# A two-layer decoder trunk: second-layer scores and transposes moved from the whole TensorE array to its 64-row halves

## The chip, the cores and the metric

The kernel runs on one core of one Trainium2 chip. The metric is the device time of one execution in microseconds (us), less being better. Instructions run on five engines: TensorE (PE in the profile, its weight loads PEld), VectorE (DVE), ScalarE (ACT), GpSimd (POOL) and SyncE (SP), which here issues all DMAs.

## The reference

Two layers work on 2048 tokens of width 1024, with 16 learned meta tokens in front. The first is sliding-window attention with sinks beside a convolution branch. The second, which the change is about, is stick-breaking attention with 16 heads of size 64:

```python
def stick_breaking_attention(q, k, v):
    ...
    scale = d ** -0.5
    for i in range(nb):                       # blocks of 128 queries
        kend = (i + 1) * BLOCK
        z = jnp.einsum('bqhd,bkhd->bhqk', qp[:, i * BLOCK:kend], kp[:, :kend]) * scale
        valid = (kpos >= META_PAD) & (kpos < qpos)
        log_beta = jax.nn.log_sigmoid(z)
        log_1m = jnp.where(valid, jax.nn.log_sigmoid(-z), 0.0)
        after = lax.cumsum(log_1m, axis=3, reverse=True) - log_1m
        a = jnp.where(valid, jnp.exp(log_beta + after), 0.0)
        outs.append(jnp.einsum('bhqk,bkhd->bqhd', a, vp[:, :kend]))
...
def stick_breaking_mixer(h, w_in, w_out):
    q, k, v, g = _split(h @ w_in, SB_SPLITS)
    o = stick_breaking_attention(...)
    return (o * jax.nn.silu(g)) @ w_out
```

Each layer adds its normalised output to its input.

## The kernel before

**Precision.** Matmuls take fp32 data. A large product is made of rounded parts: an operand x is split into xh (rounded, "fp32r") and the rest xl. `mm3` (lines 137 to 139) makes one product from three matmuls, xh yh + xh yl + xl yh. Projections, in both layers, are 24 matmuls for each unit of up to 512 tokens, in one PSUM bank (`pj`).

**The second layer** takes pairs of heads p = 0..7, and halves of the sequence hf = 0, 1. `proj(p, hf)` makes q, k, v and the gate for a pair and writes them to device memory; `attn(p, hf)` reads them back. `interleave` weaves the steps of `attn` for one pair into those of `proj` for a later one. Within `attn`, `start` loads k and v (tiles `kst`, `vt1`), `group` opens an accumulator `av` for 512 queries, `qload(m)` loads the queries of a pair of tiles (256 queries, `qt`), `chunk` works on one stretch of up to four key blocks for these 256 queries and both heads, and `finish` adds the meta tokens' values and multiplies by the gate.

One `chunk`, for each head h and each query tile x of 128:
- scores: head size 64 fills only half of the array's 128 rows, so `kst` holds kh in rows 0 to 63 and kl in rows 64 to 127, and `qt` holds qh twice, or ql twice. Two matmuls over all 128 rows (L928) make (qh + ql)(kh + kl) in a bank `z`;
- ScalarE makes sigmoid(-z/8) (`om`, L935) and sigmoid(z/8) (`be`, L936); VectorE forms the running product from the right (L941) and multiplies it into `be` (L942); GpSimd sets edge columns and masks;
- transposes: each 128x128 block of `be` is transposed by TensorE (L960) into a bank `pt`, four blocks to a bank; ScalarE copies the bank to `aT` (L966);
- values: `aT` is multiplied by v (L974) into `av`, head 0 in the partitions 0 to 63, head 1 in 64 to 127. As fp32 matmuls they run as two instructions each.

**PSUM.** Eight banks: PB = (2, 3, 2) for `pj`, `pz` (scores, and transposes elsewhere) and `pt`, and one for `av`. In the first layer projections alternate between `pj` and `pz`; in the second they use `pj` alone.

**What sets the order.** The program is written engine by engine by a scheduler, which simulates the program as recorded and places each instruction when its operands are due; `high_priority` moves the value matmuls forward, `issue_after` (in `behind`) holds projections behind earlier value matmuls. The engines then run in that fixed order, each waiting on semaphores. Of instructions that are recorded side by side, the one whose bank or operand is free first can come first.

Of the kernel before, what the change touches and what calls it, by code (L numbers as in the profile page):

```python
# [18 lines left out]
P = 128  # L19
# [18 lines left out]
PB = (2, 3, 2)  # L38
# [42 lines left out]
class Trunk:  # L81
# [105 lines left out]
    def layer0(self, after=None):  # L187
# [319 lines left out]
        def cbranch(ut):  # L507
# [44 lines left out]
            def pw():  # L552
# [3 lines left out]
                for m in range(4):  # L556
                    if m % 2 == 0:
                        wh, wl = self.weights(pwset, a["w_pw2"][m // 2], lambda: w2.tile([P, KB, P], F32, tag="yl", name="raw", bufs=1), f"wp{m // 2}")
                    ps = self.bank("pj", "pw")
# [87 lines left out]
        def outp(t):  # L647
# [3 lines left out]
            def mm(nh):  # L651
# [9 lines left out]
                ps = self.bank("pj", "po")  # L661
# [92 lines left out]
    def after0(self, pool, tags):  # L754
        self.layer1_pools()
        self.evs = (pool, tags, D, 2)
        self.H, self.gates, self.tags = {}, [], cycle(("raw", "wh", "wl", "wh", "wl"))
# [9 lines left out]
        def proj(p, hf, parts=(0, 1)):  # L767
# [11 lines left out]
            def unit(m, part, c0, n, evac):  # L779
                def go():  # L780
# [4 lines left out]
                    ps = self.bank("pj", "pj1")  # L785
# [54 lines left out]
    def layer1(self):  # L840
# [12 lines left out]
        def attn(p, hf):  # L853
# [43 lines left out]
            def qload(m):  # L897
                q0 = NM + m * 2 * P
                S["q"] = qs = []
                for h in range(2):  # L900
                    for i in range(2):
                        qt = w2.tile([P, 256], F32R, tag=f"q{h}{i}", name="qt")
                        for j in range(2):
                            self.mv(qt[j * HD : j * HD + HD], qd[i][p, h * HD : h * HD + HD, q0 : q0 + 256])
                        qs.append(qt)

            def pair_steps(m):
# [5 lines left out]
                def chunk(ei):  # L913
# [7 lines left out]
                    for h in range(2):  # L921
                        for x in range(2):
                            n = nbs[x] * P + mo
                            if n == 0:
                                continue
                            z = self.bank("pz", "z")
                            for i in range(2):
                                nc.tensor.matmul(z[:, :n], S["q"][2 * h + i][:, x * P : x * P + P], S["k"][h][:, k0 : k0 + n], start=(i == 0), stop=(i == 1))  # L928
# [7 lines left out]
                            nc.scalar.activation(be[:, :n], z[:, :n], AF.Sigmoid, scale=0.125)  # L936
# [11 lines left out]
                    for c in range(0, b1 - b0, 2):  # L948
                        cw = min(2, b1 - b0 - c)
                        aTs = []  # L950
                        for h in range(2):
                            pt = self.bank("pt", "pt1")
                            lo, hi = None, 0
                            for b in range(c, c + cw):
                                for x in range(2):
                                    if b < nbs[x]:
                                        o = (b - c) * 256 + x * P
                                        lo = o if lo is None else lo
                                        hi = max(hi, o + P)
                                        nc.tensor.transpose(pt[:, o : o + P], bes[h, x][:, mo + b * P : mo + b * P + P], self.ident)  # L960
                            aT = w4.tile([P, 512], F32, tag="aT", name="aT")
                            if nbs[0] < c + cw and cw == 2:
                                nc.scalar.copy(aT[:, :256], pt[:, :256])
                                cps.append(nc.scalar.copy(aT[:, 384:512], pt[:, 384:512]))
                            else:
                                cps.append(nc.scalar.copy(aT[:, lo:hi], pt[:, lo:hi]))  # L966
                            aTs.append(aT)
# [182 lines left out]
```

## Time and profile before

| | us |
|---|---|
| median of 3 runs | 2894.17 (2893.23 to 2900.21) |
| the profiled execution | 2898.19 |
| its span, first to last instruction | 2896.5 |
| TensorE busy | 2740.0 (95%) |
| VectorE busy | 2171.0 (75%) |
| ScalarE busy | 1466.1 (51%) |
| GpSimd busy | 753.9 (26%) |
| mean granted TensorE clock | 0.981 |

How to read the lines of a profile below. The page gives, for each engine, busy time, share of the span and count of instructions. A group of instructions reads: line, engine, operation, output<-inputs, partitions x elements, xcount | busy us, mean ns of one | idle time of the engine before them and what ended it. Matmuls overlap in their pipeline, so a group's count times its mean is more than its busy time; where one follows the next, the pace is the distance between their starts or ends. In the timeline a row has its start and its duration in us, and neighbours of the same kind are merged with their count. "128*128" is the part of the array that a matmul uses: rows by columns. In a row by windows come the stretch, its length, and each engine's busy us with its instructions in brackets (PE, PEld, DVE, ACT, POOL), then TensorE's granted clock, the DMA engines' busy share, and GB/s. A row of waits says who waited for whom: us in total, times, the longest.

### The profile page before, as it was taken

To read this page: it belongs to the slowest core of one execution; us is meant where nothing else is said; L and a number is where in the kernel's file an instruction comes from. 1 tells how busy PE (TensorE), PEld (TensorE's weight loads), DVE (VectorE), ACT (ScalarE), POOL (GpSimd) and SP (SyncE) were. 2 spreads that over 40 slices of the span, in tenths; PEclk is the share of its full clock that TensorE was granted. 3 is DMA by queue.
4 is the path that set the end of the run, shared out by engine and by line. 5 is a ranking of instruction groups with operands and counts; after the bars stand their busy time and mean duration, and the time that the engine had idled before them with its cause. 6 is when DMAs were issued, how large, how long until landed. Compare 5 with 4: busy or idle time off the path is not lost.

```text
span 2896.5 us, 49247 instructions
## 1 busy us (share of the span) xinstructions
PE 2740.0 (95%) x16110; PEld 2199.4 (76%) x16110; DVE 2171.0 (75%) x3448; ACT 1466.1 (51%) x3568; POOL 753.9 (26%) x2663
## 2 busy tenths in 40 slices
PE   6999899998999999999999899999999999989997
PEld 6888677876777798888887677767777777766876
DVE  4899679886757743666668987888888887887864
ACT  4211344335646323545545666666666666665551
POOL 4222201010000212333335532323233222333210
PEclk9999999999989999999999999999999999999999
DMA  6665767668757664444446462323233342243332
GB/s 243 222 206 189 233 186 232 195 216 256 224 181 203 204 195 141 136 125 129 136 134 185 126 176 74 103 80 97 68 102 92 85 111 74 73 135 121 113 95 91
DMA packets 294191, 433.49 MB, mean 150 GB/s; under 512 B 45552, under 2 KB 199552, under 8 KB 290864
## 3 DMA queue, kind: packets, MB, share of 16 engines
q1 hardware_dynamic: 293936, 430.34, 49.4%
q8 instruction: 129, 2.11, 0.3%
q14 instruction: 126, 1.03, 0.1%
HBM read 282.80 MB, written 142.14 MB: 147 GB/s over the span
## 4 chain that ended last, share of the span: by engine, by line
PE 73%; DVE 8%; DMA 6%; ACT 4%; issue 4%; POOL 2%; SPq 1%; DVEq 0%; ACTq 0%; POOLq 0%
PE pj L137 12%; PE pj L138 11%; PE pj L139 11%; PE z L928 8%; PE av L974 7%; PE pt L960 7%; PE po L137 4%; PE po L138 4%; PE po L139 4%; DVE S L941 2%; DVE y L308 1%; DVE be L942 1%; DMA qs<-qr 1%; PE av L990 1%; ACT be L936 1%
## 5 line engine op out<-in xcount | busy, mean ns | idle before, releaser
L941 DVE TENSOR_TENSOR_SCAN S<-om,be 128x401 f32<-128x401 f32 (+3 forms) x512 | 536.8, 1070 | 72.7 <-ACT om L935 51.6
L935 ACT ACTIVATE om<-z 128x384 f32<-128x384 f32 (+5 forms) x768 | 379.1, 512 | 202.0 <-PE z L928 130.3
L942 DVE TENSOR_TENSOR be<-be,S 128x385 f32<-128x385 f32 (+5 forms) x768 | 415.3, 566 | 77.3 <-POOL be L933 22.1
L137 PE MATMUL pj<-th,wh 128*128 128x512 f32 (+2 forms) x1280 | 461.2, 360 | 6.7 <-DVE ev L826 4.0
L139 PE MATMUL pj<-th,wl 128*128 128x512 f32 (+2 forms) x1280 | 454.0, 355 | 0.0
L138 PE MATMUL pj<-tl,wh 128*128 128x512 f32 (+2 forms) x1280 | 451.7, 353 | 0.0
L966 ACT COPY aT<-pt 128x512 f32<-128x512 f32 (+2 forms) x672 | 334.7, 505 | 192.8 <-PE pt L960 153.2
L928 PE MATMUL z<-kst,qt 128*128 128x384 f32 (+6 forms) x1536 | 395.5, 358 | 31.4 <-ACT be L936 30.1
L936 ACT ACTIVATE be<-z 128x384 f32<-128x384 f32 (+5 forms) x768 | 376.8, 507 | 72.7 <-PE pt L960 72.1
L960 PE MATMUL pt<-ident,be 128*128 128x128 f32 x2176 | 363.1, 281 | 19.4 <-ACT ev L815 7.7
L308 DVE SCALAR_TENSOR_TENSOR y<-u,cw,y 128x1040 f32<-128x1040 f32 (+1 forms) x240 | 339.6, 1415 | 3.4
L960 PEld LDWEIGHTS pt<-ident,be 128*128 128x128 f32 x2176 | 252.9, 141 | 114.8 <-ACT aT L966 31.7
L137 PE MATMUL pj<-hTh,wh 128*128 128x512 f32 (+2 forms) x880 | 318.0, 362 | 14.4 <-DVE gt L387 5.5
L139 PE MATMUL pj<-hTh,wl 128*128 128x512 f32 (+2 forms) x880 | 315.1, 359 | 6.5 <-POOL wl L127 5.2
L138 PE MATMUL pj<-hTl,wh 128*128 128x512 f32 (+2 forms) x880 | 315.1, 358 | 2.3 <-DVE hTl L185 2.3
L928 PEld LDWEIGHTS z<-kst,qt 128*128 128x128 f32 x1536 | 248.4, 191 | 76.0 <-ACT be L936 55.5
L974 PE MATMUL av<-aT,vt 128*64 128x256 f32 (+1 forms) x2304 | 279.1, 377 | 4.3 <-DVE og L992 4.3
L932 POOL MEMSET om<- 128x1 f32 x768 | 74.0, 98 | 772.6 <-DVE S L941 757.6
L137 PEld LDWEIGHTS pj<-th,wh 128*128 128x128 f32 x1280 | 242.3, 189 | 33.7 <-DVE ev L826 4.9
L139 PEld LDWEIGHTS pj<-th,wl 128*128 128x128 f32 x1280 | 241.3, 189 | 30.2 <-DVE wl L112 0.3
L138 PEld LDWEIGHTS pj<-tl,wh 128*128 128x128 f32 x1280 | 241.9, 189 | 25.4 <-issue 0.4
L941 DVE TENSOR_TENSOR_SCAN S<-om 128x257 f32<-128x257 f32 (+4 forms) x256 | 204.8, 811 | 62.1 <-POOL om L939 49.3
(190 smaller groups left out, 4471.3 us busy)
## 6 DMA issues: line engine op xcount, KB each, us to landing
raw<-in_w_in SPq DMA_DIRECT2D x98, 512.0 KB, 4.1
wh<-wk SPq DMA_DIRECT2D x38, 512.0 KB, 4.7
wl<-wk SPq DMA_DIRECT2D x38, 512.0 KB, 5.9
qt<-qhd SPq DMA_DIRECT2D x256, 64.0 KB, 2.6
qt<-qld SPq DMA_DIRECT2D x256, 64.0 KB, 2.4
wk<-wh SPq DMA_DIRECT2D x22, 512.0 KB, 3.2
wk<-wl SPq DMA_DIRECT2D x22, 512.0 KB, 3.8
kst<-khd SPq DMA_DIRECT2D x16, 516.0 KB, 7.2
```

The costliest lines, as they stand in the source:

```text
L137: mm(out, sh, mh, start=first, stop=False)
L138: mm(out, sh, ml, start=False, stop=False)
L139: mm(out, sl, mh, start=False, stop=last)
L308: return lambda: nc.vector.scalar_tensor_tensor(y[:, :TW], u[:, w : w + TW], cw[:, j, w : w + 1], y[:, :TW], ALU.mult, ALU.add)
L928: nc.tensor.matmul(z[:, :n], S["q"][2 * h + i][:, x * P : x * P + P], S["k"][h][:, k0 : k0 + n], start=(i == 0), stop=(i == 1))
L935: nc.scalar.activation(om[:, :n], z[:, :n], AF.Sigmoid, scale=-0.125)
L936: nc.scalar.activation(be[:, :n], z[:, :n], AF.Sigmoid, scale=0.125)
L941: nc.vector.tensor_tensor_scan(P_[:, : n + 1][:, ::-1], om[:, : n + 1][:, ::-1], om[:, : n + 1][:, ::-1], init, ALU.mult, ALU.bypass)
L942: nc.vector.tensor_tensor(bl[:, : n + 1], bl[:, : n + 1], P_[:, : n + 1], ALU.mult)
L960: nc.tensor.transpose(pt[:, o : o + P], bes[h, x][:, mo + b * P : mo + b * P + P], self.ident)
L966: cps.append(nc.scalar.copy(aT[:, lo:hi], pt[:, lo:hi]))
L974: mi = nc.tensor.matmul(av[h * HD : h * HD + HD, qc0 + x0 : qc0 + 256], S["v"][:, b0 + b, h * HD : h * HD + HD], at, start=not S["started" ...
```

## The change

In the second layer:
- *Scores.* `kst` and `qt` now hold the two heads of a pair, one in rows 0 to 63 and the other in rows 64 to 127, in two tiles each for the rounded part and the rest. A query tile's scores are three products of 64 rows for each head, qh kh + qh kl + ql kh (the product ql kl is gone), recorded with the two heads in turn, into two banks at once. The first of the six waits (`after_all`) for ScalarE's reads of the two scores that had these banks before.
- *Loads.* k comes in 2 DMAs where it took 4, q in 2 where it took 8.
- *Transposes.* A 128x128 block is transposed as two halves of 64 queries, u = 0 from rows 0 to 63 and u = 1 from rows 64 to 127, each into a bank of its own. A bank takes the halves u of all blocks of both heads of one query tile. Two copies for each query tile bring them to one tile `aT` (one buffer of 8 KB in a partition, where four of 2 KB were).
- *PSUM.* PB = (1, 4, 2): one bank for `pj`, four for `pz`. Where no attention runs beside them, second-layer projections and output products alternate between `pj` and `pz`, as do the first layer's.

```diff
-PB = (2, 3, 2)
+PB = (1, 4, 2)
...
-                    ps = self.bank("pj", "pw")
+                    ps = self.bank(next(banks), "pw")
...
-                ps = self.bank("pj", "po")
+                ps = self.bank(next(banks), "po")
...
+        self.zread, self.free = [], cycle(BK)
...
-                    ps = self.bank("pj", "pj1")
+                    ps = self.bank(next(self.free), "pj1")
...
-                for h in range(2):
+                for i in range(2):
                     kst = w4.tile([P, T], F32R, tag="kst", name="kst")
-                    for i in range(2):
-                        self.mv(kst[i * HD : i * HD + HD, :n], kd[i][p, h * HD : h * HD + HD, :n])
+                    self.mv(kst[:, :n], kd[i][p, :, :n])
                     ks.append(kst)
...
-                for h in range(2):
-                    for i in range(2):
-                        qt = w2.tile([P, 256], F32R, tag=f"q{h}{i}", name="qt")
-                        for j in range(2):
-                            self.mv(qt[j * HD : j * HD + HD], qd[i][p, h * HD : h * HD + HD, q0 : q0 + 256])
-                        qs.append(qt)
+                for i in range(2):
+                    qt = w2.tile([P, 256], F32R, tag=f"q{i}", name="qt")
+                    self.mv(qt, qd[i][p, :, q0 : q0 + 256])
+                    qs.append(qt)
...
-                    for h in range(2):
-                        for x in range(2):
-                            n = nbs[x] * P + mo
-                            if n == 0:
-                                continue
-                            z = self.bank("pz", "z")
-                            for i in range(2):
-                                nc.tensor.matmul(z[:, :n], S["q"][2 * h + i][:, x * P : x * P + P], S["k"][h][:, k0 : k0 + n], start=(i == 0), stop=(i == 1))
+                    for x in range(2):
+                        n = nbs[x] * P + mo
+                        if n == 0:
+                            continue
+                        zs, wait = [self.bank("pz", "z") for _ in range(2)], self.zread[-4:-2]
+                        for i, j in ((0, 0), (0, 1), (1, 0)):
+                            for h in range(2):
+                                r = slice(h * HD, h * HD + HD)
+                                mi = nc.tensor.matmul(zs[h][:, :n], S["q"][i][r, x * P : x * P + P], S["k"][j][r, k0 : k0 + n], start=(i + j == 0), stop=(i == 1))
+                                if i + j + h == 0:
+                                    self.after_all(mi, wait)
+                        for h in range(2):
+                            z = zs[h]
...
-                            nc.scalar.activation(be[:, :n], z[:, :n], AF.Sigmoid, scale=0.125)
+                            self.zread.append(nc.scalar.activation(be[:, :n], z[:, :n], AF.Sigmoid, scale=0.125))
...
-                    for c in range(0, b1 - b0, 2):
...
+                    aT = w2.tile([P, 2, 2, 2, 4, 64], F32, tag="aT", name="aT", bufs=1)
+                    for x in range(2):
+                        nb = nbs[x]
+                        if nb == 0:
+                            continue
+                        pts = [self.bank("pt", "pt1").rearrange("p (h b q) -> p h b q", h=2, b=4) for _ in range(2)]
                         for h in range(2):
...
+                            for b in range(nb):
+                                o = mo + b * P
+                                for u in range(2):
+                                    r = slice(u * 64, u * 64 + 64)
+                                    nc.tensor.transpose(pts[u][:, h, b], bes[h, x][r, o : o + P], self.ident[r, r])
+                        for u in range(2):
+                            cps.append(nc.scalar.copy(aT[:, x, u, :, :nb], pts[u][:, :, :nb]))
+                    for b in range(b1 - b0):
+                        x0 = 0 if b < nbs[0] else 1
+                        avs += [(h, b, x0 * P, aT[:, x0:, :, h, b].rearrange("p x u q -> p (x u) q")) for h in range(2)]
...
-                ps = self.bank("pj", "po1")
+                ps = self.bank(next(self.free), "po1")
...
+        self.free = cycle(("pj",))
         for p in range(2, 6):
             interleave(proj(p, 0), attn(p - 2, 0))
...
+        self.free = cycle(BK)
         for t in range(8, NT):
```

The scheduler writes a new order for all engines. Two places on TensorE's queue, in the second half of the second layer. First, where scores stand among a projection's matmuls (`pj1`), before: all rows use the whole array.

```order
L138 MATMUL pj1_22379<-tl1_17660,wh1_22252 128x512
L139 MATMUL pj1_22379<-th1_17659,wl1_22253 128x512
L928 MATMUL z_22336<-kst_21198,qt_21953 128x400
L928 MATMUL z_22336<-kst_21198,qt_21956 128x400
L960 MATMUL pt1_22214<-ident_60,be_22170 128x128
L960 MATMUL pt1_22214<-ident_60,be_22182 128x128
L960 MATMUL pt1_22214<-ident_60,be_22170 128x128
L960 MATMUL pt1_22214<-ident_60,be_22182 128x128
L928 MATMUL z_22432<-kst_21195,qt_22420 128x256
L928 MATMUL z_22432<-kst_21195,qt_22423 128x256
```

And the like of it now (`z_26338` and `z_26339` are the two heads' banks):

```order
L139 MATMUL pj1_26409<-th0_17353,wl1_26406 128x512
L137 MATMUL pj1_26409<-th0_17353,wh1_26405 128x512
L927 MATMUL z_26338<-kst_25725,qt_26114 128x384
L927 MATMUL z_26339<-kst_25725,qt_26114 128x384
L927 MATMUL z_26338<-kst_25727,qt_26114 128x384
L927 MATMUL z_26339<-kst_25727,qt_26114 128x384
L927 MATMUL z_26338<-kst_25725,qt_26116 128x384
L927 MATMUL z_26339<-kst_25725,qt_26116 128x384
L138 MATMUL pj1_26409<-tl0_17354,wh1_26405 128x512
L139 MATMUL pj1_26409<-th0_17353,wl1_26406 128x512
```

The six 64-row matmuls stand in the midst of a projection that uses 128 rows, with the heads in turn as they were recorded. Second, transposes beside value matmuls, before (`be_22194` and `be_22206` are two query tiles of a head):

```order
L974 MATMUL av1_21945<-aT_22149,vt1_21201 64x256
L974 MATMUL av1_21945<-aT_22156,vt1_21201 64x256
L960 MATMUL pt1_22221<-ident_60,be_22194 128x128
L960 MATMUL pt1_22221<-ident_60,be_22206 128x128
L960 MATMUL pt1_22221<-ident_60,be_22194 128x128
L960 MATMUL pt1_22221<-ident_60,be_22206 128x128
L928 MATMUL z_22464<-kst_21198,qt_22426 128x256
L928 MATMUL z_22464<-kst_21198,qt_22429 128x256
```

And now, with `pt1_26045` the bank of the halves u = 0 and `pt1_26046` that of u = 1, `be_25997` and `be_26007` the two heads:

```order
L962 MATMUL pt1_26045<-ident_60,be_25997 128x64 x3
L962 MATMUL pt1_26045<-ident_60,be_26007 128x64 x3
L970 MATMUL av1_25741<-aT_25902,vt1_25729 64x256 x8
L962 MATMUL pt1_26046<-ident_60,be_25997 128x64 x3
L962 MATMUL pt1_26046<-ident_60,be_26007 128x64 x3
L927 MATMUL z_26247<-kst_25725,qt_26114 128x384
L927 MATMUL z_26248<-kst_25725,qt_26114 128x384
```

The code records the halves u = 0 and u = 1 of a block side by side; in the queue all six of u = 0 come first, then value matmuls of the chunk before, then the six of u = 1.

More of the change, by code (lines that the diff above doesn't have):

```diff
@@ L947, in chunk @@
                     cps, avs = [], []
-                    for c in range(0, b1 - b0, 2):
-                        cw = min(2, b1 - b0 - c)
-                        aTs = []
-                        for h in range(2):
[L952 to L967, printed above, removed]
-                        for b in range(c, c + cw):
-                            o = (b - c) * 256
-                            x0 = 0 if b < nbs[0] else P
-                            avs += [(h, b, x0, aTs[h][:, o + x0 : o + 256]) for h in range(2)]
```

## Prediction

> **What bounds the kernel now.** I read the busy line and the chain of the page first, then the second layer by windows, since the change touches only that layer's work.
>
> ```profile
> span 2896.5 us, 49247 instructions
> PE 2740.0 (95%) x16110; PEld 2199.4 (76%) x16110; DVE 2171.0 (75%) x3448; ACT 1466.1 (51%) x3568; POOL 753.9 (26%) x2663
> PE 73%; DVE 8%; DMA 6%; ACT 4%; issue 4%; POOL 2%; SPq 1%; DVEq 0%; ACTq 0%; POOLq 0%
> ...
> 1968.60:2098.50 129.90, 125.47 (x755) 93.17 (x754) 107.64 (x141) 87.48 (x211) 38.18 (x180) 1.00 0.32 90
> ...
> 1057.00:2896.50 1839.50, 1762.35 (x10806) 1387.39 (x10804) 1370.33 (x1948) 1046.69 (x2650) 589.31 (x2396) 0.99 0.39 113
> ```
>
> TensorE is busy 95% of the span and carries 73% of the chain. The second layer runs from 1057 to the end: 1839.5 us with TensorE idle for 77. One stage of its second half (one pair of heads, 129.9 us) has TensorE at 125.5, VectorE at 107.6 and ScalarE at 87.5. So TensorE bounds it, and what the change does to TensorE's own time there is the sum; nothing else is within 20 us of being the limit of a stage.
>
> **The change part by part.** Three kinds of matmul are priced first.
>
> ```profile
> L928 PE MATMUL z<-kst,qt 128*128 128x384 f32 (+6 forms) x1536 | 395.5, 358 | 31.4 <-ACT be L936 30.1
> L960 PE MATMUL pt<-ident,be 128*128 128x128 f32 x2176 | 363.1, 281 | 19.4 <-ACT ev L815 7.7
> L960 PEld LDWEIGHTS pt<-ident,be 128*128 128x128 f32 x2176 | 252.9, 141 | 114.8 <-ACT aT L966 31.7
> L928 PEld LDWEIGHTS z<-kst,qt 128*128 128x128 f32 x1536 | 248.4, 191 | 76.0 <-ACT be L936 55.5
> ...
> 1803.47 1.04 PE L960 MATMUL pt<-ident,be 128*128 128x128 f32 x8
> ...
> 2021.34 1.52 PE L974 MATMUL av<-aT,vt 128*64 128x256 f32 x12
> 2022.79 0.66 PE L960 MATMUL pt<-ident,be 128*128 128x128 f32 x4
> ...
> 2025.60 1.05 PE L990 MATMUL av<-amT,zvm 128*128 128x128 f32 x8
> 2026.49 0.60 PE L960 MATMUL pt<-ident,be 128*128 128x128 f32 x4
> ```
>
> Busy times overlap in the pipeline, so I price by pace. Eight transposes take 1.04 us, four take 0.60: 0.11 each. That gives 2176 x 0.11 = 239 us now.
>
> *Do two halves of the array run side by side?* The trace shows it for halves by columns: eight 128-column matmuls of L990 take 1.05 us, 0.11 each, so twelve of 256 columns would need 2.6 us one after another; the value matmuls L974, whose two heads write the two column halves in turn, take 1.52. Halves by rows no row of before shows. I take it that they too overlap when neighbours in the queue belong to different halves, since the nearest row says so; the other end is no overlap at all.
>
> *Scores (gain).* Columns that TensorE streams for them:
>
> ```profile
> L928 PE MATMUL z<-kst,qt 128*128 128x384 f32 x512 | 138.8, 365 | 10.4 <-ACT be L936 9.9
> L928 PE MATMUL z<-kst,qt 128*128 128x400 f32 x320 | 89.0, 371 | 9.4 <-ACT be L936 9.3
> L928 PE MATMUL z<-kst,qt 128*128 128x512 f32 x256 | 84.4, 423 | 4.7 <-ACT be L936 4.2
> L928 PE MATMUL z<-kst,qt 128*128 128x256 f32 x224 | 50.6, 307 | 3.4 <-ACT be L936 3.4
> L928 PE MATMUL z<-kst,qt 128*128 128x272 f32 x160 | 34.6, 313 | 3.3 <-ACT be L936 3.3
> L928 PE MATMUL z<-kst,qt 128*128 128x144 f32 x32 | 6.2, 267 | 0.2 <-DMA kst<-kld 0.2
> L928 PE MATMUL z<-kst,qt 128*128 128x128 f32 x32 | 5.9, 260 | 0.0
> ```
>
> Counts times widths are 565,248 columns. A 512-column matmul follows the next after 0.23 us (368.13 and 368.36 in the fence below), so they cost 254 us. Now two heads need three pairs where they needed four matmuls; in the order all but a few score matmuls stand with the two heads in turn. Three quarters: 190 us, **-64**. Without overlap it is one and a half times: +127.
>
> *Transposes (no gain).* 2176 become 4352 of half the moving columns. Were neighbours of different halves, a pair would cost what one half costs. But in the order the scheduler has sorted them by bank: all of one half, then all of the other, often with the value matmuls between. Of 4352, only 427 pairs of neighbours (854) can overlap; 3498 stand next to their own half. The price of one then:
>
> ```profile
> 735.32 0.60 PE L182 MATMUL tp<-ident,xs 16*128 16x16 f32 x7
> ...
> 368.13 0.39 PE L138 MATMUL pj<-hTl,wh 128*128 128x512 f32 x1
> 368.36 0.39 PE L139 MATMUL pj<-hTh,wl 128*128 128x512 f32 x1
> 368.68 0.23 PE L481 MATMUL pt_m<-ident,pmc 16*128 16x16 f32 x1
> 368.84 0.50 PE L138 MATMUL pj<-hTl,wh 128*128 128x512 f32 x1
> 369.18 0.40 PE L139 MATMUL pj<-hTh,wl 128*128 128x512 f32 x1
> ```
>
> The nearest row is L182 for the 16 meta tokens: 16 rows of the array, 128 stationary columns, 16 moving. Seven take 0.60 us, a lone one (L481) 0.23: (0.60 - 0.23) / 6 = 0.062 each, though the moving part is an eighth; the weight load paces it. I take 0.062; the lower end is half of 0.11, the upper end 0.062 too unless rows add to the load. (3498 + 427) x 0.062 = 243 against 239: **+4**, with -23 at the lower end.
>
> *Changes of the array's mode (loss).* Four transposes after L974 end at 2022.79 + 0.66 = 23.45, 0.59 us after the last value matmul (2021.34 + 1.52); four after L990, which uses the whole array, end 0.44 after it (27.09 against 26.65). A change of column mode costs 0.15. Row mode is in the trace too: L481 uses 16 rows. The projection before it ends at 368.75, L481 at 368.91 (0.16, against a pace of 0.06), the projection behind it at 369.34: 0.43 later instead of 0.23. So entering costs 0.10 to 0.15 and going back to a wide weight load 0.20. Before, the second layer changes mode 384 times (into and out of value matmuls), 375 x 0.15 + 9 x 0.20 = 58 us. In the new order score and transpose groups are 64-row islands between projections and value matmuls: 1135 changes, 655 into transposes, values and other narrow loads x 0.15, 480 into scores, projections and meta values x 0.20: 194 us. **+136**; at 0.10 each it would be +55.
>
> The Trainium skill, "TensorEngine Tiling (Array Packing)", Key Properties, says that changing the tiling mode, as opposed to the tile, drains TensorE; the rows agree, at 0.10 to 0.20 us. It gives no figure for that; by the twofold speedup of its Overview alone, an estimate would book 239 / 2 + 64 us of gain and end near 2710, by the rows the sum is the one below.
>
> *Scores right behind a half transpose (loss).* A score's weight load takes 191 ns, a transpose's 141. The 50 ns more were covered by a 0.11 us transpose and are not by 0.062; the order has 225 such places: **+11** (0 to 11).
>
> *Waits.*
>
> ```profile
> PEld z L928 <- ACT be L936: 55.5, 103, 2.8
> PEld pt L960 <- ACT aT L966: 31.7, 102, 2.1
> ...
> 1277.64 0.40 PE L139 MATMUL pj<-th,wl 128*128 128x512 f32 x1
> 1278.08 0.59 ACT L798 CAST ev<-pj 128x512 fp32r<-128x512 f32 x1 [1.44 <-PE pj L139]
> 1278.70 0.69 DVE L799 TENSOR_TENSOR ev<-pj,ev 128x512 fp32r<-128x512 f32 x1 [3.38 <-ACT ev L798]
> ```
>
> Score weight loads wait 55.5 us for ScalarE to free a bank. Now one wait, for both heads' banks, stands at the head of six score matmuls where each head had its own; all of TensorE is queued behind it, as before. There are half as many such heads, and four banks instead of three: I take half away, **-27** (0 to -55). Projections keep one bank: the next unit waits for the evacuation, 1.35 us from the end of L139 (1278.04) to the end of L799 (1279.39). Between two units the order leaves other TensorE work; priced as above, 31 of 153 places have less than 1.4 us, 13 us short together: **+13**, and 52 if VectorE's queue adds 1 us. Transposes wait 31.7 us for copies of their bank. Now the second query tile waits for both banks of the first, but the scores of the next group mostly stand between: 0, at most +32. The single aT tile holds what four held, since value matmuls stand before the next copies already: 0.
>
> *Beside other work, at nothing:* 416 fewer DMA issues on SP's queue and half the q and k bytes (DMA is 32% busy in the stage, and the chain has 1% of SPq); the copies to aT, 736 before and 768 now, of the same elements in all (ScalarE has 42 us to spare in the stage); first-layer banks, where projections alternate between one pj and four pz.
>
> Sum: -64 + 4 + 136 + 11 - 27 + 13 = +73. The profiled execution took 2898.2 us beside its 2896.5 span, 4.0 above the median shown; 2894.2 + 73 = **2967**.
>
> **The rivals.**
> 1. *Faster: half transposes at half load.* If a load of 64 rows took half of 0.062, whatever the order, they would cost 122 us, not 243: -48 in all, 2846. For it: no row has 64 rows. Against it: 16 rows already take 0.062. It decides from 0.043 us a half downwards.
> 2. *No change: the drains fall into idle time.* TensorE idles 77 us in the second layer; drains that run while it would wait anyway cost nothing. At best 73 - 77 = -4: 2890. Against it: the changes of column mode cost their 0.15 in the rows above while waiting for nothing.
> 3. *More waits than I charge.* One projection bank at 52 (+39) and both-bank waits at 32: +144, 3038.
> 4. *The score pairs don't overlap by rows.* +127 instead of -64: +264, 3158. The Trainium skill, "TensorE: Matmul & The Clock Gate", Part 3, reports 3.07 times for four row tiles, which speaks against it; the column halves of this trace agree, no row here shows row halves. The same part says that matmuls are never reordered, by which sorted halves can't overlap; the order of L974 and its neighbours in the trace agrees.
>
> **How the numbers follow.** My forecast (2915 to 3010) 0.56; rival 3 0.12, rival 4 0.10, rival 2 0.09, rival 1 0.13. The range 2860 to 3045 leaves out rival 4 and half of rival 1. Runs of before lie 0.24% apart, so 0.3%, 8.7 us, is what can be told from no change. Faster 0.13, same 0.09, slower 0.78; the forecast's own range has one sign.
>
> **What would show it.** Score pairs (now L927) starting a few ns apart and busy time near three quarters; half transposes (L962) at about 0.06 us each in runs, with the total of a stage not below 20 us; about 50 more mode changes in a stage of the second half, each with 0.15 to 0.2 us in front of the next matmul; such a stage at 130 to 136 us, VectorE still near 108. I am wrong if transposes of one half start less than 0.045 us apart, if the matmul behind a 64-row group ends on its usual pace, or if score pairs follow one another at full length.

## The result, and the profile after

The changed kernel takes 2968.3 us, the median of 4 runs (2966.8 to 2968.9), and the kernel before on the same chip 2897.1 (2893.2 to 2900.2). The ratio is 1.025, with a 95% interval of 1.0238 to 1.0263: 71 us slower. 2967 were forecast, in a range of 2860 to 3045. The profiled run took 2968.9 us. The top of its page and the chain's shares by engine:

```profile
span 2966.9 us, 54530 instructions
PE 2788.5 (94%) x19054; PEld 2177.0 (73%) x19054; DVE 2155.2 (73%) x3448; ACT 1453.7 (49%) x3596; POOL 728.6 (25%) x2663
PE 71%; DVE 8%; ACT 7%; DMA 6%; issue 4%; POOL 2%; SPq 1%; DVEq 0%; ACTq 0%; POOLq 0%
```

Then two windows in the same columns as those of before (start:end, length, and the busy time of PE, PEld, DVE, ACT and POOL; then granted clock, DMA share, GB/s): one stage of the second half of the second layer, and the layer from its first score matmul to the end.

```profile
2420.80:2556.10 135.30, 127.86 (x1021) 91.55 (x1019) 107.11 (x141) 86.84 (x210) 35.37 (x181) 0.99 0.24 79
...
1108.30:2966.90 1858.60, 1765.85 (x13400) 1320.07 (x13399) 1350.02 (x1934) 1033.83 (x2656) 562.75 (x2392) 0.98 0.31 99
```

A stage takes 135.3 us where it took 129.9, with VectorE still at 107. The first score matmul comes 51 us later than before, because with `pj` and `pz` in turn about 53 us of second-layer projections moved ahead of it. So neither the layer's start nor its length can be compared alone. What can be is the start of the first score plus TensorE's busy time behind it, and beside that TensorE's idle time behind it. Before: 1057.0 + 1762.4 = 2819.4, and 77.1 idle. After: 1108.3 + 1765.9 = 2874.2, and 92.7 idle. TensorE works 55 us more, and idles 16 us more: 71. (Of the 55, 22 are work at a lower clock, as the table of the experiments shows.)

The groups of the changed kernel that answer to those shown of before:

```profile
L962 PEld LDWEIGHTS pt<-ident,be 64*128 64x128 f32 x4352 | 292.2, 139 | 170.2 <-issue 90.6 <-ACT aT L964 50.7 <-ACT ev L816 9.2
L927 PEld LDWEIGHTS z<-kst,qt 64*128 64x128 f32 x2304 | 214.3, 188 | 49.2 <-issue 33.2 <-ACT be L939 5.3 <-ACT aT L964 1.8
...
L927 PE MATMUL z<-kst,qt 64*128 64x384 f32 (+6 forms) x2304 | 332.9, 364 | 0.0
```

Its waits (total us, times, longest):

```profile
PE pt L962 <- ACT aT L964: 25.9, 55, 3.6
...
PEld av L970 <- ACT aT L964: 35.8, 82, 0.7
...
ACT be L939 <- PE pt L962: 188.7, 88, 5.8
```

And of before, two waits and a group that the prediction did not show:

```profile
PEld av L974 <- ACT aT L966: 8.4, 32, 0.4
...
ACT be L936 <- PE pt L960: 72.1, 58, 3.4
```

```profile
L137 PEld LDWEIGHTS pj<-th,wh 128*128 128x128 f32 x1280 | 242.3, 189 | 33.7 <-DVE ev L826 4.9 <-POOL wh L111 2.5 <-POOL om L932 0.6
```

Scores have nearly stopped waiting for ScalarE (5.3 us at their loads, from 55.5). Transposes and value matmuls wait for the copies instead: 50.7 from 31.7, and 35.8 from 8.4. In between, ScalarE's sigmoid (`be`) waits longer for transposes to read the buffer that it is to write.

The prices can be read from one stretch of TensorE's queue:

```profile
2278.35 0.58 PE L962 MATMUL pt<-ident,be 64*128 64x64 f32 x6
2278.87 0.50 PE L137 MATMUL pj<-th,wh 128*128 128x512 f32 x1
2279.30 0.96 PE L927 MATMUL z<-kst,qt 64*128 64x512 f32 x6
2280.19 0.50 PE L138 MATMUL pj<-tl,wh 128*128 128x512 f32 x1
2280.53 0.40 PE L139 MATMUL pj<-th,wl 128*128 128x512 f32 x1
```

Ends, start plus length: 2278.93, 2279.37, 2280.26, 2280.69, 2280.93. The projection behind six halves ends 0.44 after them, where its pace is 0.23 (the last two rows: 0.24): 0.21 for the change of mode. Six scores of 512 columns end 0.89 after it: three pairs at 0.23 and 0.20 for the change. The projection behind them comes 0.43 later: 0.20 again. And six halves of one bank take 0.58 us: 0.27 for the first and 0.062 for each of the others. Over the second layer of this trace the median change costs the same: 0.14 into halves, 0.20 into scores and projections.

### The profile page after: what moved, and what is told of

It reads as the page before. It is cut to its first block, busy times and chain, and to the rows that moved or that the text cites. A ratio compares the mean times of both kernels' runs of the same rounds, so it can differ in the third digit from the quotient of the medians.

```text
span 2966.9 us, 54530 instructions
## 1 busy us (share of the span) xinstructions
PE 2788.5 (94%) x19054; PEld 2177.0 (73%) x19054; DVE 2155.2 (73%) x3448; ACT 1453.7 (49%) x3596; POOL 728.6 (25%) x2663
## 4 chain that ended last, share of the span: by engine, by line
PE 71%; DVE 8%; ACT 7%; DMA 6%; issue 4%; POOL 2%; SPq 1%; DVEq 0%; ACTq 0%; POOLq 0%
PE pj L137 11%; PE pj L139 10%; PE pj L138 10%; PE av L970 9%; PE z L927 6%; PE pt L962 6%; PE po L137 4%; PE po L139 4%; PE po L138 4%; DVE y L308 3%; ACT aT L964 3%; ACT be L939 2%; ACT om L938 1%; PE av L986 1%; PE s L457 1%
## 5 line engine op out<-in xcount | busy, mean ns | idle before, releaser
L944 DVE TENSOR_TENSOR_SCAN S<-om,be 128x401 f32<-128x401 f32 (+3 forms) x512 | 528.0, 1062 | 37.3 <-issue 16.5
L939 ACT ACTIVATE be<-z 128x384 f32<-128x384 f32 (+5 forms) x768 | 391.4, 510 | 188.8 <-PE pt L962 188.7
L964 ACT COPY aT<-pt 128x384 f32<-128x384 f32 (+3 forms) x768 | 358.5, 478 | 217.6 <-PE pt L962 112.2
L962 PEld LDWEIGHTS pt<-ident,be 64*128 64x128 f32 x4352 | 292.2, 139 | 170.2 <-issue 90.6
L938 ACT ACTIVATE om<-z 128x384 f32<-128x384 f32 (+5 forms) x768 | 347.0, 507 | 112.7 <-PE z L927 48.9
L962 PE MATMUL pt<-ident,be 64*128 64x64 f32 x4352 | 361.0, 232 | 37.0 <-ACT aT L964 25.9
L927 PE MATMUL z<-kst,qt 64*128 64x384 f32 (+6 forms) x2304 | 332.9, 364 | 0.0
L970 PE MATMUL av<-aT,vt 128*64 128x256 f32 (+1 forms) x2304 | 293.3, 392 | 22.3 <-ACT aT L964 20.2
L927 PEld LDWEIGHTS z<-kst,qt 64*128 64x128 f32 x2304 | 214.3, 188 | 49.2 <-issue 33.2
L970 PEld LDWEIGHTS av<-aT,vt 128*64 128x64 f32 x2304 | 154.1, 141 | 109.9 <-ACT aT L964 35.8
```

The source lines that it names most:

```text
L927: mi = nc.tensor.matmul(zs[h][:, :n], S["q"][i][r, x * P : x * P + P], S["k"][j][r, k0 : k0 + n], start=(i + j == 0), stop=(i == 1))
L938: nc.scalar.activation(om[:, :n], z[:, :n], AF.Sigmoid, scale=-0.125)
L939: self.zread.append(nc.scalar.activation(be[:, :n], z[:, :n], AF.Sigmoid, scale=0.125))
L944: nc.vector.tensor_tensor_scan(P_[:, : n + 1][:, ::-1], om[:, : n + 1][:, ::-1], om[:, : n + 1][:, ::-1], init, ALU.mult, ALU.bypass)
L962: nc.tensor.transpose(pts[u][:, h, b], bes[h, x][r, o : o + P], self.ident[r, r])
L964: cps.append(nc.scalar.copy(aT[:, x, u, :, :nb], pts[u][:, :, :nb]))
```

## The experiments

Eleven kernels were run. Each time is a median, each ratio against the kernel before on the same chip. The table uses one profiled execution of each: TensorE's work is the start of the first score matmul plus TensorE's busy time behind it, against 2819.4 of before; idle is the rest of the window, against 77.1. The column between them is explained below the table. Busy time counts the tails of the pipeline, so it is a rougher measure than the pace of instructions.

| kernel | time, us | ratio (95%) | TensorE's work | of it half clock | idle |
|---|---|---|---|---|---|
| after | 2968.3 | 1.025 (1.0238-1.0263) | +55 | +22 | +16 |
| banks alone | 2935.6 | 1.0137 (1.012-1.0155) | +12 | +16 | +28 |
| scores, no halves | 3009.2 | 1.0394 (1.0375-1.0412) | +57 | +21 | +53 |
| halves alone | 3003.9 | 1.0376 (1.0361-1.0392) | +130 | +17 | -26 |
| layout alone | 2908.0 | 1.0041 (1.0029-1.0053) | +5 | +4 | +5 |
| 16-row transposes added | 3013.0 | 1.0398 (1.0383-1.0414) | +158 | -2 | -43 |
| whole transposes added | 2932.5 | 1.0125 (1.0109-1.0141) | +64 | -3 | -28 |
| one score matmul | 2861.9 | 0.9883 (0.9864-0.9901) | -75 | +25 | +45 |
| halves in pairs | 2987.5 | 1.0318 (1.0294-1.0342) | -15 | +68 | +110 |
| pairs, ten `be` | 3037.5 | 1.0486 (1.047-1.0502) | -9 | +88 | +153 |
| pairs, banks 1, 2, 4 | 3206.6 | 1.1072 (1.1053-1.1091) | +149 | +130 | +160 |
| banks 2, 3, 2 | 3032.3 | 1.0477 (1.0455-1.0498) | +72 | +35 | +47 |

The clock is the part of TensorE's work that the prediction left out. In the second layer the granted clock is 0.50 in some stretches, most of them of 3.4 or 6.8 us, and 1.00 elsewhere: 7 stretches, 32 us in all, before, and 16, 81 us, in the changed kernel. One of its 16 runs from 2207.0 to 2210.4:

```profile
2201.04 1.52 PE L970 MATMUL av<-aT,vt 128*64 128x256 f32 x12
...
2206.00 0.30 PE L982 MATMUL ptm<-ident,am 128*128 128x128 f32 x1 [0.49 <-ACT aT L964]
2206.78 2.64 PE L970 MATMUL av<-aT,vt 128*64 128x256 f32 x12 [0.48 <-ACT aT L964]
```

Twelve value matmuls of one shape take 1.52 us ahead of it and 2.64 where all but the first 0.2 us lies in it. Half of TensorE's busy time in such stretches is lost by the clock: 12 us before, 34 in the changed kernel. The column has each kernel's loss against those 12. The stretch above follows 3.4 us in which TensorE idled for 1.0, in pieces of at most 0.49, and kernels that idle more mostly have more such stretches; that idling brings them on was not tried.

### What does a change of mode cost on the end? Two additions to the kernel before

Ahead of each of 704 banks of transposes, one more transpose: of 16 rows in one kernel, of the whole array in the other. Its output is overwritten.

```diff
                             pt = self.bank("pt", "pt1")
+                            nc.tensor.transpose(pt[:, :16], self.ident[:16], self.ident[:16, :16])
```

> The kernel before with one extra transpose ahead of each of the 704 banks of second-layer transposes, which uses 16 rows of the array: 1408 more mode changes and nothing else. Its result is overwritten by the transposes behind it. Theory (a change of mode costs on the path): 704 x (0.10 into it + 0.06 + 0.15 behind it) = 220 us on TensorE, less up to 75 us of it that runs where TensorE waited anyway: 145 to 220 us slower, 3040 to 3115, and 100 to 150 us above the next kernel. Rival (drains fall into idle time): within 30 us of the next kernel.

```diff
                             pt = self.bank("pt", "pt1")
+                            nc.tensor.transpose(pt[:, :P], self.ident, self.ident)
```

> The same extra instruction in the same 704 places, as a transpose over the whole array: no change of mode. 704 x 0.11 = 77 us on TensorE. Both theories: 0 to 77 us slower than before, 2896 to 2973, by how much of it runs where TensorE waited anyway; it is the control of the kernel with the drains.

Measured: 3013.0 and 2932.5. TensorE's timeline of the first kernel, then the layer's window in the first and in the second:

```profile
2100.66 0.39 PE L137 MATMUL pj<-th,wh 128*128 128x512 f32 x1
2100.98 0.23 PE L953 MATMUL pt<-ident 16*128 16x16 f32 x1
2101.14 0.66 PE L961 MATMUL pt<-ident,be 128*128 128x128 f32 x4
2101.72 0.23 PE L953 MATMUL pt<-ident 16*128 16x16 f32 x1
```

```profile
1056.00:3011.20 1955.20, 1921.53 (x11506) 1461.31 (x11504) 1363.14 (x1948) 1062.92 (x2650) 582.08 (x2396) 0.99 0.37 107
```

```profile
1059.00:2932.70 1873.70, 1824.21 (x11505) 1461.64 (x11504) 1367.90 (x1948) 1054.13 (x2650) 580.21 (x2396) 0.99 0.38 111
```

The 16-row transpose ends 0.16 after the projection, the four whole ones 0.59 after it, of which 0.44 is their pace: 0.15 going back. So the prices of a change in the queue are the ones that I used, 0.10 into 16 rows (0.16 less a pace of 0.06) and 0.15 back. There are 1260 more changes (1644 in this trace against 384): 704 into the 16-row transposes and 704 out of them, less 148 at 0.15 that they replace. Less 0.05 for each of 704 smaller transposes, that is about 119 us of TensorE's queue more than in the second kernel, and the two differ by 80. The second kernel needs no more changes of mode than before: 704 x 0.11 = 77 us of plain work, and +35 in time. So 115 of 196 us came out at the end in the first, and 35 of 77 in the second. The windows show where a part of the rest went: TensorE's idle time fell from 77 us to 34 in the first and to 49 in the second. My theory (3040 at least for the first) was too high, and the rival that drains cost next to nothing (30 us at most) was too low by far.

### Work taken away

The second of the two score matmuls is left out, so that the queries' remainders do not count.

```diff
-                            for i in range(2):
-                                nc.tensor.matmul(z[:, :n], S["q"][2 * h + i][:, x * P : x * P + P], S["k"][h][:, k0 : k0 + n], start=(i == 0), stop=(i == 1))
+                            nc.tensor.matmul(z[:, :n], S["q"][2 * h][:, x * P : x * P + P], S["k"][h][:, k0 : k0 + n], start=True, stop=True)
```

> The kernel before with the second of the two score matmuls left out (the rounded queries alone are used, ql is dropped from the scores): 129 us less of TensorE's own work, nothing else changed, no change of mode added. It tells what TensorE time is worth when it is taken away. Theory (about half of TensorE's time in the second layer is on the path, as the added transposes showed): 45 to 75 us faster than before, 2822 to 2852. Rival (TensorE alone bounds the layer): 115 us or more, 2780 or less.

Measured: 2861.9, 35 us faster with half of the scores' 254 us gone, and less than both had said. Its window of the layer, then two waits:

```profile
1057.00:2866.70 1809.70, 1687.75 (x10076) 1295.21 (x10075) 1378.24 (x1949) 1040.81 (x2654) 585.38 (x2397) 0.98 0.40 115
```

```profile
PEld z L927 <- ACT be L935: 65.0, 125, 4.5
...
PEld pt L959 <- ACT aT L965: 56.3, 116, 1.6
```

TensorE has 75 us less to do by its busy time and idles 45 us more. What it saves, it spends on waiting, most of it for ScalarE (65.0 from 55.5 and 56.3 from 31.7), and on the half clock, which takes 25 us more of its busy time than before. By pace, a microsecond of TensorE removed was worth 0.27 here (35 of 127), though TensorE was busy 95% of the span. This is the only kernel that beats the one before, and it computes less.

### The parts of the change, one at a time

*Banks alone.* The kernel before with PB = (1, 4, 2) and the banks in turn, with its own scores and transposes.

```diff
-PB = (2, 3, 2)
+PB = (1, 4, 2)
...
-                    ps = self.bank("pj", "pj1")
+                    ps = self.bank(next(self.free), "pj1")
```

> The kernel before with only the PSUM part of the change: one bank for projections, four for scores, and the alternation where no attention runs. 384 mode changes, as before. Theory: only the waits for the one bank, 0 to 40 us slower than before: 2895 to 2937 us. Rival (the loss is waiting for that bank): most of the 71 us, 2945 us or more.

Measured: 2935.6, +40 where the step said +13, at the upper end of the range. Two of its waits, then the group of the projections' first load:

```profile
PEld z L929 <- ACT be L937: 63.8, 109, 3.7
PEld pt L961 <- ACT aT L967: 47.0, 98, 3.1
```

```profile
L137 PEld LDWEIGHTS pj<-th,wh 128*128 128x128 f32 x1280 | 241.9, 189 | 50.5 <-issue 9.0 <-DVE ev L800 5.6 <-POOL wh L111 4.7
```

Idle time ahead of the projections' first loads grew by 17 us, which is about what I had priced. The rest shows where I had charged nothing: score loads wait 8 us longer for ScalarE, transposes 15 us longer for copies. The fourth score bank did not shorten the scores' wait in this kernel. TensorE's work at full clock is no more than before (+12, of it 16 by the half clock). What in the new order causes the later copies stays open.

*Halves alone.* The kernel before with only the half transposes and their copies; banks as before.

```diff
+                                for u in range(2):
+                                    r = slice(u * 64, u * 64 + 64)
+                                    nc.tensor.transpose(pts[u][:, h, b], bes[h, x][r, o : o + P], self.ident[r, r])
```

> The kernel before with only the transposes in halves (scores over the whole array, banks as before). 1384 mode changes; 477 pairs of neighbours, 3398 halves alone. Theory: transposes +3, changes +176: about 3075 us, 3040 to 3110. Rival (waiting for the one projection bank is the loss, halves and changes are free): within 20 us of before, 2880 to 2915 us.

Measured: 3003.9. The rival, within 20 us of before, is refuted, and my own range is missed on its low side: with 1384 changes of mode against 384, TensorE's work grows by 130 us (113 at full clock), and 26 us of its idle time took up a part. The copies are hardly at fault. A kernel that has whole transposes in the new layout (one bank for a query tile and a head, one `aT` tile) shows it:

```diff
+                        for h in range(2):
+                            pt = self.bank("pt", "pt1").rearrange("p (b q) -> p b q", b=4)
+                            for b in range(nb):
+                                o = mo + b * P
+                                nc.tensor.transpose(pt[:, b], bes[h, x][:, o : o + P], self.ident)
+                            cps.append(nc.scalar.copy(aT[:, x, h, :nb], pt[:, :nb]))
```

> The kernel before with whole transposes and whole-array scores, but with the changed kernel's order of banks and copies: all blocks of one query tile and head go to one bank, two copies a query tile, one aT tile. TensorE's own work and the 384 mode changes stay as before. Theory (the changed kernel's way of copying does not itself wait more): within 25 us of before, 2870 to 2920. Rival (one aT tile and copies by query tile are part of the loss): 2930 or more.

Measured: 2908.0, ratio 1.0041 (1.0029 to 1.0053): 11 to 12 us, a ninth of the halves' price.

*Scores, no halves.* The changed kernel with the whole transposes, copies and `aT` tiles of before:

```diff
-                                    nc.tensor.transpose(pts[u][:, h, b], bes[h, x][r, o : o + P], self.ident[r, r])
...
+                                        nc.tensor.transpose(pt[:, o : o + P], bes[h, x][:, mo + b * P : mo + b * P + P], self.ident)
```

> The changed kernel with the transposes of before (whole 128x128 blocks, four aT buffers); scores in 64-row halves. 1074 mode changes against 384 before. Theory: scores -64, changes +129 (187 against 58 us), so 2950 to 2990 us: the scores' part alone loses. Rival (drains fall into idle time; the sorted halves are the whole loss): -64 and little against it, about 2835 to 2860 us.

Measured: 3009.2. Both missed, the rival by far: its scores alone do not gain. They put +74 on top of the banks. A score group among whole transposes changes mode on both sides (1074 changes), and transposes wait much longer for copies (47.0 at their loads with the banks alone):

```profile
PEld pt L963 <- ACT aT L969: 71.8, 100, 4.1
PE pt L963 <- ACT aT L969: 44.9, 40, 3.9
```

The halves, which cost 108 us alone, then save 41 when they join the scores. Next to the score groups the halves bring only 61 more changes of mode (1135 against 1074), where alone they bring 1000. Why this kernel's copies are later than those of the changed one is not shown.

### Would the halves pay if they ran in pairs?

In the changed kernel the scheduler sorts the halves by bank. Here the first half of a query tile waits for the last two copies out of the banks, so both banks are free and all 2176 pairs stand side by side.

```diff
+                                    if h + b + u == 0:
+                                        self.after_all(mi, self.tread[-2:])
```

> The changed kernel, with one thing added: the first half transpose of a query tile waits for the copies out of both banks, so that the queue holds all 4352 halves in neighbouring pairs (2176 pairs, none alone; 1014 mode changes). Theory (halves sorted by bank don't overlap, each mode change costs 0.15 to 0.20 us): 2176 x 0.062 = 135 us of transposes instead of 243 and 121 fewer changes (-20), so -128 against the changed kernel, less what the added wait costs: 2840 to 2880 us. Rival (the loss is waiting, for the one projection bank and for both transpose banks): the added wait makes it worse, 2968 to 3000 us.

Measured: 2987.5, so the theory fell and the rival held. TensorE's timeline first, then waits:

```profile
2290.97 0.39 PE L139 MATMUL pj<-th,wl 128*128 128x512 f32 x1
2291.29 0.59 PE L962 MATMUL pt<-ident,be 64*128 64x64 f32 x12
2291.81 0.50 PE L137 MATMUL pj<-th,wh 128*128 128x512 f32 x1
```

```profile
PEld av L973 <- ACT aT L966: 86.2, 85, 2.6
PEld pt L962 <- ACT aT L966: 79.2, 82, 3.9
...
ACT be L939 <- PE pt L962: 415.5, 221, 7.6
```

The array does what it can: twelve halves take 0.59 us, as long as six of one bank in the changed kernel. Halves of different rows overlap fully, halves of the same rows not at all. TensorE has 70 us less to do than in the changed kernel, and idles 94 us more. At full clock it would have 116 less, near the 128 that the theory gave the pairs; the half clock takes 46 of them back, and the idle time the other 70 and 24 more. It waits for copies, and ScalarE's sigmoid waits 415.5 us for transposes (188.7 in the changed kernel, 72.1 before). TensorE and ScalarE now wait for each other in turn.

The first remedy tried gives the sigmoid's output ten buffers in one ring:

```diff
-                            bl = w2.tile([P, 513], F32, tag=f"be{h}{x}", name="be")
+                            bl = w2.tile([P, 513], F32, tag="be", name="be", bufs=10)
```

> The kernel with the halves in pairs, and ten buffers for the weights be in one ring, where each of the four (head, tile) had two of its own. 929 mode changes; TensorE's own work by the rates is 16 us less than in the kernel with the pairs, 144 less than in the changed kernel. Theory (the pairs gained their 108 us on TensorE and lost them to a ring of waits in which the sigmoid be waits for the transposes that still read its buffer): the waits shrink, 2900 to 2960. Rival (the pairs wait for the two transpose banks and the copies, whatever the buffers of be): 2960 to 2985.

Measured: 3037.5, above what both said.

```profile
ACT be L939 <- PE pt L962: 301.1, 152, 7.6
PEld pt L962 <- ACT aT L966: 102.8, 81, 4.8
PEld av L973 <- ACT aT L966: 92.3, 92, 1.8
```

The sigmoid waits less, and TensorE more. So more buffers moved the wait and did not end it. The second remedy gives four banks to transposes and two to scores, and moves both waits to fit (against the kernel with the pairs):

```diff
-PB = (1, 4, 2)
+PB = (1, 2, 4)
...
-                        zs, wait = [self.bank("pz", "z") for _ in range(2)], self.zread[-4:-2]
+                        zs, wait = [self.bank("pz", "z") for _ in range(2)], self.zread[-2:]
...
-                                        self.after_all(mi, self.tread[-2:])
+                                        self.after_all(mi, self.tread[-4:-2])
```

> The kernel with the halves in pairs, with four banks for transposes and two for scores (one for projections): pairs of halves have two sets of banks, score pairs one. 2163 pairs, 1011 mode changes, TensorE's own work as with the pairs. Theory (the pairs of halves wait for both their banks): TensorE's waits for copies fall by half or more, but score pairs now wait for ScalarE; 2930 to 3010, so about as slow as the kernel with the pairs. Rival (the waits are for VectorE and for the copies' own time, not for banks): waits for copies stay above 100 us, 3010 or more.

Measured: 3206.6, far above the theory; the rival had a time of 3010 or more, but by waits for copies. The wait is for other things:

```profile
PE pt L962 <- DVE be L945: 154.6, 142, 4.2
...
PEld pt L962 <- DVE be L945: 88.2, 81, 2.5
PEld z L927 <- ACT be L939: 64.3, 74, 1.9
```

No wait for copies is left among TensorE's large ones, but transposes wait for their input from VectorE. I take it that scores with only two banks come too late for it; that was not tried apart. The granted clock is 0.934 in this run and 0.974 in the changed kernel's: of TensorE's work of +149 in the table, 130 are the half clock.

*Three score banks.* The changed kernel with PB = (2, 3, 2) and the scores' wait moved to fit:

```diff
-PB = (1, 4, 2)
+PB = (2, 3, 2)
...
-                        zs, wait = [self.bank("pz", "z") for _ in range(2)], self.zread[-4:-2]
+                        zs, wait = [self.bank("pz", "z") for _ in range(2)], self.zread[-3:-1]
```

> The changed kernel with the banks of before, two for projections and three for scores; the scores' first wait is for the reads that three banks call for. 1178 mode changes, TensorE's own work by the rates of the prediction 4 us less. Theory (one projection bank costs some 40 us by waits and order, four score banks gain back about as much): 2945 to 2985. Rival (the one bank is a net loss in the changed kernel too): 2920 to 2940.

Measured: 3032.3, 64 us above the changed kernel, and above what both had said. Score matmuls wait again:

```profile
PEld z L927 <- ACT be L939: 50.2, 75, 2.5
PE z L927 <- ACT be L939: 38.4, 70, 2.3
```

With both heads' scores at once, the second `pj` bank does not pay for the score bank that is lost. So the move of the bank costs 40 us alone, and without it the rest of the change is slower still.

## Why the prediction was right, and which of its terms were not

The time and the sign came out; so did the prices of instructions. The path to the sum did not, in places that cancelled.

- **Scores, -64: price right.** Six scores of 512 columns take three paces of 0.23. The busy time that I had named as a sign fell to 332.9 of 395.5, 0.84 and not three quarters, since a busy row counts each pipeline tail. Of 1152 pairs, 692 start within 0.02 us of each other; where a score starts among halves the two heads fall out of step, as below. Rival 4 (no overlap) is refuted.
- **Transposes, +4: price right.** 0.062 for a half next to its own half, one price for two next to each other. Rival 1 (a half load at half the price) is refuted. The trace has 622 pairs of halves that start within 0.02 us of each other, where I had counted 427: 12 us less than the term. What I did not foresee is that a half also runs beside a score matmul. This and the next step are read from the timeline:

```profile
2433.58 0.52 PE L962 MATMUL pt<-ident,be 64*128 64x64 f32 x5
2433.88 0.44 PE L927 MATMUL z<-kst,qt 64*128 64x384 f32 x1
2433.94 0.34 PE L962 MATMUL pt<-ident,be 64*128 64x64 f32 x3
2434.09 0.59 PE L927 MATMUL z<-kst,qt 64*128 64x384 f32 x4
2434.51 0.21 PE L962 MATMUL pt<-ident,be 64*128 64x64 f32 x1
2434.53 0.34 PE L927 MATMUL z<-kst,qt 64*128 64x384 f32 x1
```

Eight halves run from 2433.58 to 2434.28, 0.70 us, which is 0.27 and seven times 0.062: the score that starts among them delays them by nothing. But the scores gain nothing by it: the sixth ends at 2434.87, 0.59 after the last of these halves, and three pairs of 384 columns need 0.52 at a pace of 0.23 for 512. In 13 places of the trace three halves, a score, three halves and five scores stand by themselves, and each takes 0.05 to 0.07 us longer than its halves and score pairs one after another. Of the other stretches with halves among scores most are longer too, and ten are 0.06 to 0.09 shorter. So hardly any gain from this overlap is shown.
- **Scores right behind a half, +11: price about right.** They can start beside it, as the same rows show, but the 0.05 to 0.07 us of those 13 places is what I had charged for each.
- **Mode changes, +136: price right, worth wrong.** 0.15 and 0.20 stand in the rows above. (The Trainium skill, "TensorEngine Tiling (Array Packing)", Key Properties, says that a change of tiling mode drains TensorE; these rows agree and give it a price.) But the sum took each us of TensorE's queue as a us of the end. Added work came out at 0.45 (whole transposes) and two thirds (the drains alone, 80 of 119). Rival 2, that drains fall into idle time, was thus true in part; I had it at all or nothing. And the lower end, +55, was a slip: it has the new changes at 0.10 each but the old ones still at 58 us; with both at 0.10 it is +75.
- **Waits of scores, -27: mis-sized.** They fell by 50 us, from 55.5 to 5.3 at the loads, near the end of my range. **Waits for copies, 0: wrong.** Transposes +19 and values +27 at their loads. Together these waits change by about nothing, not by -27.
- **The clock: left out.** It takes 22 us more of TensorE's busy time than before, and the sum had no term for it.
- **One projection bank, +13: mis-sized.** The banks alone cost 40, of which up to 16 are the clock. My method, counting places with too little work between two projections, saw only the 17 us that show at the projections; rival 3 had the size, not the place.

In the sum, TensorE's work was to grow by 87 and grew by 55 in busy time, of which 33 are work at full clock; waits were to fall by 14 and idle time grew by 16. So TensorE's own work came out 54 us below the sum, and the half clock (22) and the waits (30) made up for it. Of the 54, the pairs of halves explain 12; the rest stays open, since busy time is a rough measure. The single parts do not add up either: banks +40 and halves +108 make 148, before the scores gain anything, against 71 measured. So the agreement within 2 us is luck in its last 50 us. The sign, slower because 64-row islands among 128-row work cost more than score pairs save, is shown by the halves alone (+108), by the scores without halves (+74 over the banks) and by the added drains (+80).

The stage was 135.3 us (130 to 136 foretold), VectorE 107 (near 108).

## What to carry to other kernels

Price a change on the busiest engine by pace, then ask how much of it reaches the end: in this kernel with TensorE at 95%, added work counted half to two thirds and removed work a quarter, in one or two kernels each. What TensorE saved turned into waits for copies and scores' banks and into a halved clock; so read the granted clock of a window beside its busy time. A smaller tile of the array saves TensorE time only where its matmuls stand next to work of the other half in the queue, and not as islands among work of the whole array; look at the scheduled order, not at the order in which the code records them. Before taking a buffer from one stage for another, run that move alone, and the rest without it: here the move alone cost 40 us, and the rest without it 135.

## What the runs showed of the hardware that was not expected

- Matmuls of different kinds overlap across the row halves: a score matmul starts in the midst of a run of half transposes, and these keep their 0.062 us (eight in 0.70 us). The scores end no sooner for it (0.59 us after the last half, for 0.52 of work).
- Two half transposes of different rows cost what one costs: twelve in 0.59 us where six of the same rows take 0.58. A half of 64 rows goes at the pace of the 16-row transposes (0.062), though it moves four times the columns.
- The granted clock falls to 0.50 for stretches of mostly 3.4 or 6.8 us, in one case after 3.4 us in which TensorE idled for 1.0 in pieces of at most 0.49. Its mean was 0.981 before, 0.974 in the changed kernel, 0.959 with halves in pairs and 0.934 in the slowest kernel; in the second layer that took 12, 34, 80 and 142 us of TensorE's busy time. What sets the stretches off was not tried.
